# Two transformer blocks on one core: score and meta-key products padded to 128 rows, stick-breaking scores from fp32r parts

## The chip, the cores and the metric

The kernel runs on one core of a Trainium2 chip. The metric is the device time of one execution in microseconds; three executions of the kernel before are given. TensorE is called PE in the profile, its weight loads PEld, VectorE DVE, ScalarE ACT, GpSimd POOL and SyncE SP.

## The reference

512 tokens of 1024 features go through two layers of a first block and one layer of a second one. All is float32.

```python
for l in range(2):                                   # block 1, 16 meta tokens ahead of the 512
    hn = rmsnorm(h, norm_gain[l]); proj = hn @ w_in[l]
    # four heads of two maps (64 features each): a = softmax(q0 k0) - lam * softmax(q1 k1); do = a @ v
    do = rmsnorm(diff_attention(dq, dk, dv, lam, chunk_ids), subln_gain[l]) * (1 - lam_init) * silu(dg)
    # eight heads of 64 features, scores plus cumulated log-sigmoids of a forget gate, causal
    fo = forgetting_attention(fq, fk, fv, cum_logf, positions) * silu(fg)
    h = h + concat([do, fo]) @ w_out[l]
x = rmsnorm(h, final_gain)[:, 16:]
x = x + 0.5 * swiglu(rms_norm(x))                    # block 2
h = rms_norm(x) @ w_in_2
o_nsa = gate0 * compressed + gate1 * selected + gate2 * window    # eight query heads, two key heads
z = q_s @ k_s.T / 8                                  # stick-breaking, eight heads
a = where(mask, exp(log_sigmoid(z) + suffix sums of log_sigmoid(-z)), 0); o_sb = a @ v_s
x = x + concat([o_nsa, o_sb]) @ w_out_2
x = x + memory_cross_attention(rms_norm(x), rms_norm(mem), ...)   # 256 memory rows, four heads
x = x + 0.5 * swiglu(rms_norm(x))
```

At 512 tokens the 8 selection blocks are all selected, so the selected and the window branch are both plain causal attention here.

## The kernel before

Activations lie feature-major in eight tiles `h` of 128 features by tokens. A large product takes both operands in two fp32r parts, high and low, and adds three passes into one bank of PSUM (`dense`, `dense_tok`). The weights come through `Stream`: a DMA on SP's queue, the high part by ScalarE (L131), the low part by VectorE (L132).

Attention is put between the large products by a clock of TensorE work (`mm` and `tr` add to `self.clock`; `at` and `soon` give a step a due time; `poll` and `wait` emit it). `pump` emits one step of attention and asks for the next after a delay in proportion to its cost, at least `MIN_STEP` or `MIN_STEP2`. A step `a` makes the scores of a tile of 128 queries and their exponentials, `b` or `fl` follows about `LAT_AB` later with the transposes on TensorE, `pv` about `LAT_BC` after that with the products with the values. The order that results is scheduled once more against a simulated time line when the program is built, and is then fixed on each engine.

Scores of a head (`qk`) are two fp32r products over operands that `stack` makes. For head h of a pair, the queries are a tile of 128 rows, the high parts in the head's own 64 rows and the low parts in the other 64; the keys are a tile with the high parts in the own 64 rows and the key as it is in the others. The second product adds the high parts of the queries with the low parts of the keys, over the head's own 64 rows alone:

```python
own = slice(64 * h, 64 * h + 64)
q = Q[0][h]
self.mm(out, q[(slice(None), *qc)], K[0][h][(slice(None), *kc)], True, False)
self.mm(out, q[(own, *qc)], K[1][(own, *kc)], False, stop)
```

In block 1 (`layer`) the scores of a query tile have 16 + 128(t+1) keys, at least 256 columns where 128 queries are in work; the tile t = 3 is cut in two halves of 264 (`scores`). The causal masks are added by a bfloat16 product with the identity, the forget gate's sums by a bfloat16 product of `sel` and `ck` over 72 rows. The transposed probabilities of the 16 meta keys stand in a tile `PTm` of 16 rows, the values in `Vm`, and `pv` begins with their product. The mixer does selected and window attention (`nsa_steps`, keys `nk` and `nkl`), then stick-breaking (`sb_steps`). Its scores are one f32 product over 64 rows of the pair's queries and keys (L1501), which runs as two passes; tanh, a reversed running product on VectorE (L1509) and one more VectorE operation (L1511) make the weights. Each pair's steps may begin when its own keys and queries are there. While they run, TensorE also does the output products of the first half of the heads. The attention over the memory (`memory`) uses `qk` with keys `mk` and `mkl` from `memory_operands`.

Of the kernel before, what the change touches and what calls it, by code (L numbers as in the profile page):

```python
# [11 lines left out]
F32 = mybir.dt.float32  # L12
# [28 lines left out]
T = 512  # L41
# [59 lines left out]
def layer_order(l):  # L101
    """products of a layer of block 1 in their order"""
    o = []
    gates = [(u + "g", i) for u, i in UNITS]
    for n, (u, i) in enumerate(UNITS):
        o += [(u + x, i) for x in "vkq"]
        for _ in range((GA0, GA1)[l][n]):
            o.append(gates.pop(0))
    return o + [("o", d) for d in range(KD)]


class Stream:
    """Weights in the order of their use: loaded and split into two float32r parts a few chunks ahead."""
# [30 lines left out]
def weight_plan(A):  # L144
    plan = []

    def cut(key, src, cols, rows=None):
        """[rows, cols] of src"""
# [55 lines left out]
class Prep:  # L204
    """The operands of the products after an rms norm: X = h*gain in two parts, R = 1/rms on every partition."""
# [7 lines left out]
    def split(self, d, a=None, b=None):  # L213
        """X of feature tile d, columns a:b of its tokens"""
# [7 lines left out]
class Net:  # L222
# [14 lines left out]
    # ---- PSUM tiles, one bank each  # L237
# [12 lines left out]
    # ---- order of emission: chains of small steps are placed between the large products by a clock of PE time  # L250
# [4 lines left out]
    def soon(self, delay, pri, fn):  # L255
        """at, with the instructions of fn ahead of their place by pri"""
# [15 lines left out]
    def feed(self, items, interval):  # L272
        """emit items (ready, fn) one after another, each interval(i) after the one before"""
# [17 lines left out]
    # ---- TensorE  # L291
# [17 lines left out]
    def dense(self, ps, m, W, c0, X, seg, ks=None):  # L309
        """ps[m, tokens] = W^T X, three passes over the parts; ks: only these row tiles"""  # L310
# [12 lines left out]
    def dense_tok(self, ps, Ws, c0, n, X, t0):  # L323
        """ps[tokens t0.., n] = X^T W over the chunks Ws of rows"""
# [14 lines left out]
    # ---- small arithmetic  # L339
# [15 lines left out]
    def stacks(self, pool, tag, shape, keys, bufs=2):  # L355
        """tiles for the operands of two heads: queries [high; low], keys [high; high], and the low parts of keys"""
        S = [pool.tile([128, *shape], F32R, tag=f"{tag}{h}", name=f"{tag}{h}", bufs=bufs) for h in range(2)]
        return S, pool.tile([128, *shape], F32R, tag=tag + "l", name=tag + "l", bufs=bufs) if keys else None

    def stack(self, dst, src, cut):  # L360
        """two heads of 64 features of src into the tiles of stacks, at cut(tile)"""
        nc, v = self.nc, self.nc.vector
        S, L = dst
        for h in range(2):
# [5 lines left out]
            v.tensor_tensor(out=cut(S[h])[other] if L is None else cut(L)[own], in0=src[own], in1=hi.bitcast(F32),  # L370
                            op=ALU.subtract)

    def qk(self, out, Q, K, h, qc, kc, stop):
        """out = q k^T for head h, queries qc, keys kc"""
        own = slice(64 * h, 64 * h + 64)
        q = Q[0][h]
        self.mm(out, q[(slice(None), *qc)], K[0][h][(slice(None), *kc)], True, False)
        self.mm(out, q[(own, *qc)], K[1][(own, *kc)], False, stop)

    def rsqrt(self, dst, ms, n, p=128):  # L380
        """dst = 1/sqrt(ms) for [p, n]: a first guess from the bits, a step of third order, one of second"""
# [15 lines left out]
    def colsum(self, ps, parts, chunks, off):  # L397
        """ps[tokens, chunk] = sums over partitions of the parts"""
# [12 lines left out]
    def spread(self, r, chunks, R, off):  # L411
        """R [128, tokens]: r [tokens of a chunk, chunk] on every partition"""
# [10 lines left out]
    # ---- set up: constants, gains, residual  # L423
    def setup(self):
# [21 lines left out]
        with self.tc.tile_pool(name="setup", bufs=1) as sp:  # L446
# [19 lines left out]
            # rms of the tokens of block 1, from the rows as they came  # L466
# [56 lines left out]
            with self.tc.issue_after(self.ins[S_LATE]):  # L523
# [10 lines left out]
                # -lambda of each layer, on every partition  # L534
# [15 lines left out]
    # ---- rms norm of the residual, built up feature tile by feature tile  # L550
# [28 lines left out]
    def norm_end(self, P, token_r=None):  # L579
        """chain of the statistics; token_r: [128, 4] for 1/rms with tokens on partitions"""  # L580
# [50 lines left out]
    # ---- block 1  # L631
    def layer(self, l, P, nxt):
# [5 lines left out]
        with ExitStack() as st:  # L638
# [5 lines left out]
            self.ck = np_.tile([72, TT], BF16, name="ck")  # L644
            swap = list(range(8, 16)) + list(range(0, 8)) + list(range(16, 32))
            done = {}
# [19 lines left out]
            def proj(kind, u, i):  # L666
# [17 lines left out]
                dst = self.stacks(ap, "p" + kind, [TT], kind == "k")  # L684
# [3 lines left out]
            def values(u, i, vT):  # L688
                V = ap.tile([128, 4, 128], F32, tag="V", name="V", bufs=2)
                Vm = ap.tile([16, 128], F32, tag="Vm", name="Vm", bufs=2)  # L690

                def flip_v():
# [6 lines left out]
                    nc.scalar.copy(Vm, ps[:16, :128])  # L699
# [1196 lines left out]
```

## Time and profile before

| | |
|---|---|
| runs | 1974.67, 1979.1, 1981.31 us; median 1979.1 |
| span of the profiled execution, first to last instruction | 1969.9 us |
| its own time | its device time is not given beside the span; the median of the runs is 9.2 us above the span |
| TensorE busy | 1929.5 us (98%), 11075 matmuls |
| weight loads busy | 1553.2 us (79%) |
| VectorE busy | 1159.0 us (59%) |
| ScalarE busy | 846.4 us (43%) |
| GpSimd busy | 0.7 us |
| mean granted TensorE clock | 0.992 |

The stages follow from the names of the tiles: attention of layer 0 from 67 to 374 us, of layer 1 from 453 to 733, the first feed-forward from 857 to 1175, the mixer's projections to 1290, selected and window attention to 1437, stick-breaking to 1516, attention over the memory from 1546 to 1592, the second feed-forward from 1620. In a row of the timeline the columns are start and duration in us, engine, line, operation, output<-inputs, for TensorE rows times columns of the weights, then the moving operand, and a count; an fp32r operand is shown as f32. Matmul durations overlap, since the ends are modelled; the distance of two starts tells what a product keeps TensorE for. In rows of groups by line the columns are busy time, mean duration, idle time before and what ended it. L293 is the call of the matmul in `mm`, L306 the one in `tr`.

### The profile page before, as it was taken

To read this page: it belongs to the slowest core of one execution; us is meant where nothing else is said; L and a number is where in the kernel's file an instruction comes from. 1 tells how busy PE (TensorE), PEld (TensorE's weight loads), DVE (VectorE), ACT (ScalarE), POOL (GpSimd) and SP (SyncE) were. 2 spreads that over 40 slices of the span, in tenths; PEclk is the share of its full clock that TensorE was granted. 3 is DMA by queue.
4 is the path that set the end of the run, shared out by engine and by line. 5 is a ranking of instruction groups with operands and counts; after the bars stand their busy time and mean duration, and the time that the engine had idled before them with its cause. 6 is when DMAs were issued, how large, how long until landed. Compare 5 with 4: busy or idle time off the path is not lost.

```text
span 1969.9 us, 28237 instructions
## 1 busy us (share of the span) xinstructions
PE 1929.5 (98%) x11075; PEld 1553.2 (79%) x11075; DVE 1159.0 (59%) x2637; ACT 846.4 (43%) x1874; POOL 0.7 (0%) x6
## 2 busy tenths in 40 slices
PE   6999999999999999999999999999999999999999
PEld 5888888797888767888888888976665688888887
DVE  4976655458775547663443557865676665344353
ACT  4555565535555555432222233435566443222222
POOL 0000000000000000000000000000000000000000
PEclk9999999999999999999999999999999799999999
DMA  8665541176574312333333335320010123333332
GB/s 140 67 66 50 60 44 44 44 80 69 57 62 59 52 33 81 103 108 96 97 96 94 89 93 162 84 67 23 22 44 12 33 71 89 97 96 96 93 88 87
DMA packets 259439, 145.21 MB, mean 74 GB/s; under 512 B 9242, under 2 KB 256604, under 8 KB 259308
## 3 DMA queue, kind: packets, MB, share of 16 engines
q1 hardware_dynamic: 259308, 143.42, 35.7%
q8 instruction: 87, 1.43, 0.3%
q14 instruction: 44, 0.36, 0.1%
HBM read 141.30 MB, written 2.10 MB: 73 GB/s over the span
## 4 chain that ended last, share of the span: by engine, by line
PE 92%; DMA 4%; DVE 2%; ACT 1%; issue 0%; SPq 0%; DVEq 0%; ACTq 0%
PE mm L293 68%; PE s L293 12%; PE po L293 7%; PE pt L306 5%; DMA w<-in_w_in_dram 2%; PE pt L293 1%; DMA CS<-in_c_shape_dram 1%; DMA xs<-in_x_dram 1%; DVE wlo L132 0%; DMA gc<-in_nsa_kc_norm_dram 0%; DMA gr<-in_ffn_norm_dram 0%; ACT whi L131 0%; ACT L738 0%; DVE rp L661 0%; SPq L1157 0%
## 5 line engine op out<-in xcount | busy, mean ns | idle before, releaser
L131 ACT ACTIVATE whi<-w 128x1024 fp32r<-128x1024 f32 (+2 forms) x253 | 263.1, 1042 | 589.9 <-PE mm L293 504.8
L132 DVE TENSOR_TENSOR wlo<-w,whi 128x1024 fp32r<-128x1024 f32 (+2 forms) x253 | 303.6, 1201 | 76.8 <-ACT whi L131 75.6
L293 PE MATMUL mm<-actl,whi 128*128 128x512 f32 x352 | 139.4, 397 | 0.0
L293 PE MATMUL mm<-acth,wlo 128*128 128x512 f32 x352 | 139.3, 397 | 0.0
L293 PE MATMUL mm<-acth,whi 128*128 128x512 f32 x352 | 139.2, 397 | 0.0
L734 DVE TENSOR_REDUCE nm<-s 128x1 f32<-128x264 f32 (+4 forms) x171 | 69.1, 408 | 79.3 <-PE s L293 78.5
L1090 DVE SCALAR_TENSOR_TENSOR h<-mm,h 128x512 f32<-128x512 f32 x48 | 33.0, 691 | 138.0 <-PE mm L293 138.0
L738 ACT ACTIVATE P<-s,nm 128x264 f32<-128x264 f32 (+4 forms) x171 | 78.0, 458 | 72.6 <-DVE nm L734 47.9
L306 PE MATMUL pt<-ident,P 128*128 128x128 f32 (+2 forms) x588 | 97.6, 277 | 1.8 <-DVE P L1511 1.5
L1078 DVE TENSOR_TENSOR u<-mm,R 128x512 f32<-128x512 f32 x42 | 29.0, 691 | 108.6 <-PE mm L293 108.6
L293 PE MATMUL mm<-cl,whi 128*128 128x264 f32 (+1 forms) x256 | 88.2, 345 | 0.1
L293 PE MATMUL mm<-ch,wlo 128*128 128x264 f32 (+1 forms) x256 | 87.2, 343 | 0.5 <-DVE wlo L132 0.5
L293 PE MATMUL mm<-ch,whi 128*128 128x264 f32 (+1 forms) x256 | 85.8, 350 | 1.3 <-ACT ch L937 0.7
L1071 DVE TENSOR_TENSOR g<-mm,R 128x512 f32<-128x512 f32 x42 | 29.0, 690 | 89.3 <-PE mm L293 89.3
L293 PEld LDWEIGHTS mm<-acth,wlo 128*128 128x128 f32 x352 | 66.4, 189 | 15.9
L293 PEld LDWEIGHTS mm<-actl,whi 128*128 128x128 f32 x352 | 66.4, 189 | 15.9
L293 PEld LDWEIGHTS mm<-acth,whi 128*128 128x128 f32 x352 | 66.4, 189 | 15.8
L293 PE MATMUL mm<-x0h,whi 128*128 128x512 f32 (+1 forms) x202 | 71.7, 355 | 5.0 <-ACT raw L659 3.4
L306 PEld LDWEIGHTS pt<-ident,P 128*128 128x128 f32 (+2 forms) x588 | 60.9, 131 | 18.2 <-issue 13.9
L293 PE MATMUL mm<-x1h,wlo 128*128 128x512 f32 (+1 forms) x202 | 71.6, 355 | 0.0
L293 PE MATMUL mm<-x6h,whi 128*128 128x512 f32 (+1 forms) x202 | 71.0, 352 | 0.0
L293 PE MATMUL mm<-x7h,whi 128*128 128x512 f32 (+1 forms) x202 | 71.0, 352 | 0.0
(702 smaller groups left out, 5258.8 us busy)
## 6 DMA issues: line engine op xcount, KB each, us to landing
w<-in_w_in_dram SPq DMA_DIRECT2D x84, 512.0 KB, 6.8
w<-in_ffn_wg_dram SPq DMA_DIRECT2D x44, 512.0 KB, 4.0
w<-in_ffn_wu_dram SPq DMA_DIRECT2D x44, 512.0 KB, 3.9
w<-in_ffn_wd_dram SPq DMA_DIRECT2D x32, 512.0 KB, 3.7
w<-in_w_out_dram SPq DMA_DIRECT2D x20, 512.0 KB, 3.7
w<-in_ffn_wd_dram SPq DMA_DIRECT2D x16, 384.0 KB, 3.4
xs<-in_x_dram SPq DMA_DIRECT2D x4, 512.0 KB
w1k<-in_cmp_w_k_dram SPq DMA_DIRECT2D x4, 512.0 KB, 6.9
```

The lines of the kernel that those rows point to most:

```text
L131: nc.scalar.activation(out=hi, in_=w, func=AF.Copy)
L132: nc.vector.tensor_tensor(out=lo, in0=w, in1=hi.bitcast(F32), op=ALU.subtract)
L293: self.nc.tensor.matmul(out, lhsT, rhs, start=start, stop=stop)
L306: self.nc.tensor.transpose(out, in_, self.ident[:p, :p])
L734: v.tensor_reduce(out=nm[:nq, c:c + 1], in_=s[:nq, :b - a], axis=AX.X, op=ALU.max, negate=True)
L738: nc.scalar.activation(out=P_[:nq, a:b], in_=S[c][:nq, :b - a], func=AF.Exp, bias=nm[:nq, 0:1], accum_out=ls[:nq, c:c + 1])
L1071: v.tensor_tensor(out=g, in0=pg, in1=R, op=ALU.mult)
L1078: v.tensor_tensor(out=u, in0=pu, in1=R, op=ALU.mult)
L1090: v.scalar_tensor_tensor(out=H[d], in0=ps, scalar=0.25, in1=H[d], op0=ALU.mult, op1=ALU.add)
```

## The change

- `stacks` now makes low parts of keys as two tiles, one for each head of a pair, of 128 rows each (`low_parts`); the 64 rows of the other head are set to zero once by GpSimd (`zero`). `qk` runs both products over all 128 rows.
- In `layer` these tiles, the `Vm` tiles and the `PTm` tiles are made once, two of each in turn, with 128 rows, zeroed at the layer's start; `ck` and `sel` are used with 128 rows instead of 72.
- Stick-breaking scores go through `qk`: `sb_stack` cuts a pair's keys and queries into parts, for the next pair at the second tile of the pair before, for the first pair when the stage begins. There are two sets of six tiles, one in the place of the operands x4 to x6 of the large products. The scores have at least 256 columns. All four pairs now wait for the last pair's projections.
- `dynamic_dma_scratch_size=1024` is given to the program.

Docstrings and comments go too; they are left out here.

```diff
     def stacks(self, pool, tag, shape, keys, bufs=2):
         S = [pool.tile([128, *shape], F32R, tag=f"{tag}{h}", name=f"{tag}{h}", bufs=bufs) for h in range(2)]
-        return S, pool.tile([128, *shape], F32R, tag=tag + "l", name=tag + "l", bufs=bufs) if keys else None
+        return S, self.low_parts(pool, tag, shape) if keys is True else keys or None
+
+    def low_parts(self, pool, tag, shape):
+        L = [pool.tile([128, *shape], F32R, tag=f"{tag}l{h}", name=f"{tag}l{h}", bufs=1) for h in range(2)]
+        for h in range(2):
+            self.zero(L[h][64 - 64 * h:128 - 64 * h])
+        return L
+
+    def zero(self, t):
+        self.nc.gpsimd.memset(t.bitcast(F32) if t.dtype == F32R else t, 0.0)
...
-            v.tensor_tensor(out=cut(S[h])[other] if L is None else cut(L)[own], in0=src[own], in1=hi.bitcast(F32),
+            v.tensor_tensor(out=cut(S[h])[other] if L is None else cut(L[h])[own], in0=src[own], in1=hi.bitcast(F32),
...
     def qk(self, out, Q, K, h, qc, kc, stop):
-        own = slice(64 * h, 64 * h + 64)
-        q = Q[0][h]
-        self.mm(out, q[(slice(None), *qc)], K[0][h][(slice(None), *kc)], True, False)
-        self.mm(out, q[(own, *qc)], K[1][(own, *kc)], False, stop)
+        q, at = Q[0][h][(slice(None), *qc)], (slice(None), *kc)
+        self.mm(out, q, K[0][h][at], True, False)
+        self.mm(out, q, K[1][h][at], False, stop)
...
-            self.ck = np_.tile([72, TT], BF16, name="ck")
+            self.ck = np_.tile([128, TT], BF16, name="ck")
...
+            lows = [self.low_parts(ap, f"pk{a}", [TT]) for a in range(2)]
+            vms = [ap.tile([128, 128], F32, name=f"Vm{a}") for a in range(2)]
+            ptms = [ap.tile([128, 2, 128], F32, name=f"PTm{a}") for a in range(2)]
+            for x in vms + ptms:
+                self.zero(x)
+            done = {"m": 0}
...
-                dst = self.stacks(ap, "p" + kind, [TT], kind == "k")
+                dst = self.stacks(ap, "p" + kind, [TT], lows[UNITS.index((u, i)) % 2] if kind == "k" else None)
...
-                Vm = ap.tile([16, 128], F32, tag="Vm", name="Vm", bufs=2)
+                Vm = vms[UNITS.index((u, i)) % 2]
...
-                    nc.scalar.copy(Vm, ps[:16, :128])
+                    nc.scalar.copy(Vm[:16], ps[:16, :128])
...
-                PTm = ap.tile([16, 2, 128], F32, tag="PTm", name="PTm", bufs=2)
+                PTm = ptms[done["m"] % 2]
+                done["m"] += 1
...
-                nc.scalar.copy(PTm[:, :nq], psm[:16, o:o + nq])
+                nc.scalar.copy(PTm[:16, :nq], psm[:16, o:o + nq])
...
-                    P_, ls = scores(qT, kT, hh, t, self.masks[:, 1], self.sel[:72, 2 * i + hh, :], f"P{hh}",
+                    P_, ls = scores(qT, kT, hh, t, self.masks[:, 1], self.sel[:, 2 * i + hh, :], f"P{hh}",
...
-            kS, qS = {}, {}
+            kS, qS, sets, stacked = {}, {}, [], {}
+
+            def sb_stack(p):
+                if not sets:
+                    for a in range(2):
+                        pool, tags = (self.xp, ("x4h", "x4l", "x5h", "x5l", "x6h", "x6l")) if a == 0 else \
+                            (done["tp"], [f"sb{x}" for x in range(6)])
+                        x = [pool.tile([128, T], F32R, tag=tag, name="sbs" + str(n), bufs=1) for n, tag in enumerate(tags)]
+                        for h in range(2):
+                            self.zero(x[4 + h][64 - 64 * h:128 - 64 * h])
+                        sets.append(((x[0:2], None), (x[2:4], x[4:6])))
+                Q, K = sets[p % 2]
+                self.stack(K, kS[p], lambda x: x)
+                self.stack(Q, qS[p], lambda x: x)
+                stacked[p] = Q, K
...
                 def a(t, hf):
                     n = 128 * (t + 1)
                     qc = slice(128 * t, 128 * t + 128)
-                    rows = slice(64 * hf, 64 * hf + 64)
                     s = self.ps_s()
-                    self.mm(s[:, :n], qS[p][rows, qc], kS[p][rows, :n], True, False)
+                    if t == 1 and hf == 0 and p < 3:
+                        sb_stack(p + 1)
+                    w = max(n, 256)
+                    self.qk(s[:, :w], *stacked[p], hf, [qc], [slice(0, w)], False)
...
-                    [(lambda p=p: p in qS and "tp" in done, p, sb_steps) for p in range(4)]
+                    [(lambda: 3 in qS and "tp" in done, p, sb_steps) for p in range(4)]
...
                     if make is sb_steps and i == 0:
                         done["wait"] = True
+                        sb_stack(0)
...
-    nc = bacc.Bacc("TRN2", target_bir_lowering=False, num_devices=1)
+    nc = bacc.Bacc("TRN2", target_bir_lowering=False, num_devices=1, dynamic_dma_scratch_size=1024)
```

More of the change, by code (lines that the diff above doesn't have):

```diff
@@ L643, in layer @@
             CR, SR = CS[:, 0], CS[:, 1]
-            self.ck = np_.tile([72, TT], BF16, name="ck")
+            self.ck = np_.tile([128, TT], BF16, name="ck")
             swap = list(range(8, 16)) + list(range(0, 8)) + list(range(16, 32))
-            done = {}
+            lows = [self.low_parts(ap, f"pk{a}", [TT]) for a in range(2)]
[4 more added lines that the diff above has]
+            done = {"m": 0}
             att = {}
```

## The prediction

> **What bounds the kernel now.** The page first: its span line and engine totals; then the chain that ended last, summed by line; then busy time by stage.
>
> ```profile
> span 1969.9 us, 28237 instructions
> PE 1929.5 (98%) x11075; PEld 1553.2 (79%) x11075; DVE 1159.0 (59%) x2637; ACT 846.4 (43%) x1874; POOL 0.7 (0%) x6
> ```
>
> ```profile
> by line: PE mm L293 67.6%; PE s L293 11.7%; PE po L293 6.8%; PE pt L306 5.1%; DMA w<-in_w_in_dram 2.3%; PE pt L293 0.7%; DMA CS<-in_c_shape_dram 0.6%; DMA xs<-in_x_dram 0.5%; DVE wlo L132 0.5%; issue 0.4%; DMA gc<-in_nsa_kc_norm_dram 0.3%;
> ```
>
> ```profile
> 67.00:374.00 307.00, 305.90 (x2246) 258.17 (x2244) 193.44 (x538) 170.93 (x510) 0.00 (x0) 1.00 0.44 52
> 453.00:733.00 280.00, 278.61 (x1748) 221.93 (x1746) 184.53 (x451) 153.87 (x412) 0.00 (x0) 1.00 0.47 56
> 1290.00:1437.00 147.00, 146.68 (x898) 100.04 (x897) 93.18 (x253) 76.53 (x208) 0.00 (x0) 1.00 0.12 33
> 1437.00:1516.00 79.00, 76.10 (x454) 45.47 (x454) 56.97 (x119) 47.30 (x110) 0.00 (x0) 1.00 0.09 27
> 1546.00:1592.00 46.00, 42.00 (x249) 32.23 (x249) 34.16 (x109) 25.73 (x73) 0.00 (x0) 0.78 0.01 2
> ```
>
> TensorE is on the chain for about 92% of the span (the PE entries added up, most of them products on L293). The five stage rows (length, then PE, PEld, DVE, ACT, POOL busy, clock, DMA) are the attention of layer 0, of layer 1, the selected-and-window attention, the stick-breaking attention and the attention over the memory. In the first three TensorE has no holes, VectorE is busy 63%, 66% and 63%, ScalarE 56%, 55% and 52%. So time taken off a TensorE instruction there comes off the span, until a chain through VectorE and ScalarE is late.
>
> A busy TensorE is not one at its peak, so I read the spacing of its starts, from the timeline (start, busy, then the instruction).
>
> ```profile
> 454.50 0.28 PE L293 MATMUL mm<-x7h,wlo 128*128 128x264 f32 x1
> 454.62 0.28 PE L293 MATMUL s<-pk,pq 128*128 128x256 f32 x1
> 454.82 0.38 PE L293 MATMUL s<-pkl,pq 64*128 64x256 f32 x1
> 455.14 0.23 PE L293 MATMUL s<-masks,identb 128*128 128x128 bf16 x1
> ```
>
> ```profile
> 272.89 0.39 PE L293 MATMUL s<-pkl,pq 64*128 64x264 f32 x1
> 273.20 0.29 PE L293 MATMUL s<-ck,sel 72*128 72x264 bf16 x1
> 273.24 0.37 PE L293 MATMUL s<-pk,pq 128*128 128x264 f32 x1
> 273.55 0.39 PE L293 MATMUL s<-pkl,pq 64*128 64x264 f32 x1
> 273.86 0.29 PE L293 MATMUL s<-ck,sel 72*128 72x264 bf16 x1
> 273.99 0.22 PE L293 MATMUL s<-masks,identb 128*128 128x128 bf16 x1
> ```
>
> A full-height product of 264 columns is followed after 0.12 us (454.50 to 454.62). A product that has a 64-row one behind it is followed after 0.20 (454.62 to 454.82), and the 64-row product itself after 0.32 (to 455.14; 0.31 from 273.55 to 273.86). The same price from one stretch: from 272.89 to 273.55 three products of 264 columns take 0.66 us, where three at 0.12 would take 0.36 to 0.37. So going to 64 rows and back costs 0.29 us a pair (0.08 to 0.09 in, 0.20 out). The 72-row product costs nothing of the kind: 0.13 us from 273.86 to 273.99. Where the score product follows a short one, the spacing behind it is 0.31 (273.24 to 273.55); I don't count the extra 0.11, since it comes from the short spacing ahead of it.
>
> **The change part by part.** The profile's time is the span of 1969.9; the runs have a median of 1979.1 (1974.67 to 1981.31), so 9.2 us lie between span and median. I subtract from the span and take the same amount off the median.
>
> *Low-part score products, 64 to 128 rows.* Block 1 has 2 layers x 8 units x 2 heads x 5 products with 256 columns or more = 160. The mixer has 64.
>
> ```profile
> L293 PE MATMUL s<-pkl,pq x171: 179/386/452, 67.0 to 733.2; 64*128 64x264 f32 x62, 64*128 64x256 f32 x31, 64*128 64x272 f32 x31, 64*128 64x400 f32 x31
> L293 PE MATMUL s<-nkl,nq x64: 377/411/502, 1290.5 to 1434.4; 64*128 64x256 f32 x32, 64*128 64x384 f32 x16, 64*128 64x512 f32 x16
> L293 PE MATMUL po<-PTm,Vm x144: 203/268/320, 249.6 to 752.0; 16*64 16x128 f32 x128, 16*64 16x16 f32 x16
> L293 PE MATMUL po<-Vm,PTm x72: 267/274/373, 78.2 to 623.2; 16*128 16x128 f32 x64, 16*16 16x128 f32 x8
> ```
>
> (155 of the 160 are in the first row, the other five go to a buffer of another name.) 160 x 0.29 = 46 us, 64 x 0.29 = 19 us. The number of columns does not change, so the product costs what a full-height one costs, 0.12. Bounds of a pair: nothing, if the spacing is not due to the height, and 0.38, if the 0.11 above goes too. I take 0.29, measured between like products. The 16-column pairs of the meta queries I put at 0.
>
> *Meta-key products, 16 to 128 rows.* 72 and 144 instructions; those with 128 columns are two passes of 32 and 64 products.
>
> ```profile
> 106.30 0.48 PE L293 MATMUL po<-Vm,PTm 16*128 16x128 f32 x2
> 106.71 0.94 PE L293 MATMUL po<-V,PT 128*128 128x128 f32 x6
> 107.40 0.37 PE L293 MATMUL mm<-x1l,whi 128*128 128x264 f32 x1
> ```
>
> ```profile
> 271.62 0.43 PE L293 MATMUL po<-PTm,Vm 16*64 16x128 f32 x2
> 271.98 0.66 PE L293 MATMUL po<-PT,V 128*64 128x128 f32 x8
> 272.57 0.39 PE L293 MATMUL s<-pk,pq 128*128 128x264 f32 x1
> ```
>
> Heads of two maps: the two passes take 0.41 (106.30 to 106.71); the six full-height ones behind them take 0.69 (to 107.40), 0.115 each, so two would take 0.23. With 0.09 for the way in, taken as for the 64 rows, 0.27 is saved, x 32 = 9 us. Forgetting heads have two such groups a tile, of which one stands ahead of full-height passes as here: 0.36 for two passes, against eight full-height ones in 0.59, 0.15 for two. That saves 0.21 a tile, x 32 = 7 us. The other group stands alone, and its half-width output would still change the shape of the array on both sides; I count nothing for it. Ends 0.1 and 0.4 a tile, 3 and 13 us. Together 16.
>
> *The bias product, 72 to 128 rows:* 0, by the 0.13 above. *Scratch size of dynamic DMA:* the program issues no such DMA from POOL; 0.
>
> *Stick-breaking scores.* 32 products of two f32 passes on 64 rows become 32 pairs of fp32r products of max(n, 256) columns.
>
> ```profile
> 1453.94 0.49 PE L293 MATMUL s<-sbk,sbq 64*128 64x128 f32 x2
> 1454.36 0.23 PE L293 MATMUL s<-masks,identb 128*128 128x128 bf16 x1
> ```
>
> ```profile
> 1448.07 1.12 PE L293 MATMUL s<-sbk,sbq 64*128 64x512 f32 x2
> 1449.12 0.23 PE L293 MATMUL s<-masks,identb 128*128 128x128 bf16 x1
> ```
>
> ```profile
> L367 ACT ACTIVATE mk<-mkT x2: 626/628/630, 1445.0 to 1445.7; 64x512 fp32r<-64x512 f32 x2
> L369 DVE CAST mk<-mkT x2: 422/422/423, 1445.0 to 1445.5; 64x512 fp32r<-64x512 f32 x2
> L370 DVE TENSOR_TENSOR mkl<-mkT,mk x2: 684/686/689, 1446.0 to 1446.7; 64x512 fp32r<-64x512 f32 x2
> ```
>
> ```profile
> L1406 DVE SCALAR_TENSOR_TENSOR sbk<-mm,R x4: 690/692/692, 1281.1 to 1326.0; 128x512 f32<-128x512 f32 x4
> ```
>
> Before, 0.42 us at 128 columns and 1.05 at 512; in between evenly, 0.63 and 0.84. After, twice 0.12 at 256 columns, and in proportion 0.18 and 0.24 at 384 and 512: 0.24, 0.24, 0.36, 0.48. The difference over the four tiles is 1.62, x 8 = 13 us, and the way into 64 rows adds 0.09 x 32 = 3: 16 us of TensorE time. But each of the 4 pairs now needs its operands cut: 4 casts on ScalarE (0.63), 2 copies (0.42) and 4 subtractions (0.69) on VectorE, priced by the memory's keys of the same shape: 2.5 and 3.6 us a pair, 10 and 14 us in all. VectorE is busy 57 of this stage's 79 us; with 14 more it needs 71, and 79 - 16 = 63 aren't enough. VectorE is late next, behind its scan and products, and the score products of the next pair wait for its subtractions. I put the stage at 75, a gain of 4; ends +16 (the cuts all lie in slack) and -8 (all 24 us of cuts lie in the way, less the 16). That the first pair now waits for the projections of all four costs nothing: keys and queries are made from 1281 to 1326 on, the first scores stand at 1437.
>
> *Attention over the memory:* 16 pairs, 4.6 us at 0.29.
>
> ```profile
> 1558.06 0.58 PE L293 MATMUL s<-mk,mq 128*128 128x256 f32 x1 [3.70 <-ACT Pm L1773]
> 1558.57 0.58 PE L293 MATMUL s<-mkl,mq 64*128 64x256 f32 x1
> ```
>
> ```profile
> PE s L293 <- ACT P L738: 1.7, 2, 1.4
> ```
>
> ```profile
> masks.py:197 POOL MEMSET ident<- 128x128 f32 x1 | 0.2, 204 | 0.3 <-POOLq L1884 0.3
> ```
>
> The first eight pairs end in a wait of 3.70 us for ScalarE, which eats what they save. The other eight run at the halved clock (0.51 between starts). I take 3, between 0 and 10.
>
> *Zeros on POOL:* 8 fills a layer, 2 and 2 for the other keys, 4 for stick-breaking, 24 in all. By 0.2 us for 128 columns a fill of 528 is under 1 us, so under 24 us on an engine that is busy 0.7 us and on which nothing else waits. The cover is the projections and weights ahead of each first score; without it a layer starts 1 to 2 us later. I take 0.
>
> *What is late next in blocks 1 and 2.* The steps are issued at fixed distances of TensorE work, and these shrink by 11 to 13% ((46 + 16) of 587, 19 of 147). VectorE would then be busy about 71%. At present TensorE waits little for softmax (1.7 us for the exponentials in both layers). I take 5 us of new waits, between 0 and 25.
>
> Sum: 46 + 19 + 16 + 4 + 3 - 5 = 83. Span 1969.9 - 83 = 1887; median 1979 - 83 = 1896.
>
> **The rivals.**
>
> *The chains take over.* The attention stages become bound by the way from scores over maximum, exponential and scaling back to the transposes, and half of the gain is lost: 1979 - 42 = 1937. For it: VectorE at 63% and more, and distances in the code that go with the slower TensorE. Against it: waits of a few us in 587 us of block 1's attention.
>
> *The padded product pays for its weights in the open.* A full-height product may hide its weight load less than assumed, say by another 0.09 at each of the two products. Then a pair saves 0.11, the meta products half: 25 + 8 + 4 + 3 - 1 = 39, time 1940. Against it: full-height products, each with its own weights, stand at 0.12 (454.50 to 454.62). The Trainium skill, page "TensorE: Matmul & The Clock Gate", section "Part 3: Packing small matmuls — row/col tiling", says that a weight load overlaps running matmuls only when the row groups differ; by that rule this rival would win, but the spacing of 0.12 speaks against it here.
>
> *It does not do what it says.* If the spacing comes from the accumulation or the short operands and not from the height, only stick-breaking changes: 1975, no change within what can be told (0.3%, 6 us).
>
> *Slower: the clock.* In the memory stage the mean granted clock is 0.78, and products of 256 columns stand 0.51 apart. Were the padded products, half of whose rows are zeros, to halve the clock in layer 0's attention, each us of TensorE work there would take 2; it decides from 83 us of such work on. With half of the stage's remaining 276 us it gives 1979 - 83 + 138 = 2034. Against it: the clock is 1.00 in the four stages before the memory, with 64-row products that fill half the array as well.
>
> **How the numbers follow.** Forecast 0.73, chains 0.13, weights 0.06, no effect 0.04, clock 0.04. Everything at its better end: 46 + 19 + 22 + 16 + 10 = 113, so 1866; I set the low end at 1868. The high end of 1940 takes in the two rivals that halve the gain. Faster by over 0.3%: 0.73 + 0.13 + 0.06 = 0.92; same 0.04; slower 0.04.
>
> **What would show it.** No 64-row form of the low-part products; 0.12 behind each of them at 264 columns. Layer stages near 275 and 250 us, the next near 128, stick-breaking near 75 with VectorE above 90%. PE waits for exponentials under 5 us in each layer. Wrong: spacings of 0.2 or more behind the padded products, or TensorE holes in the attention stages that add up to over 25 us.

## The result, and the profile after

| | before | after |
|---|---|---|
| median of the runs | 1979.15 us (1974.67 to 1981.31) | 1889.95 us (1888.62 to 1890.34) |
| ratio, with its 95% interval | | 0.9555 [0.9536, 0.9574] |
| span of the profiled execution | 1969.9 us | 1886.5 us |
| mean granted clock | 0.992 | 0.992 |

The forecast was 1896, range 1868 to 1940. The span fell by 83.4 us, the forecast's sum was 83. The median fell by 89, since the profiled execution of before took less than the median. After's profiled execution took 1888.62 us, 2.1 above its span; by the same distance the one of before would have taken about 1972.0, less than any of its runs shown.

Where the 83 us come from, stage by stage. A stage begins with its first score product on TensorE, layer 1 and stick-breaking where the row above them ends; it ends with the start of its last product of one kind. For a layer and the memory that is the last output product (a layer is attention and the products around it), for selected and window attention the last score product, for stick-breaking the last product with the values. "Mixer start" goes from the last product of the first feed-forward to the first compression product. Columns to the right are the experiments below that move most.

| us | before | after | forecast of the difference | measured | only scores padded | only meta padded | stick-breaking as before | cuts once |
|---|---|---|---|---|---|---|---|---|
| start | 66.9 | 68.4 | 0 | +1.5 | 68.2 | 67.3 | 67.8 | 67.4 |
| layer 0 | 351.6 | 321.0 | both layers: -57 | -30.6 | 327.9 | 344.5 | 320.6 | 319.9 |
| layer 1 | 366.2 | 334.6 | | -31.6 | 345.2 | 358.7 | 334.9 | 334.9 |
| mixer start | 31.0 | 26.4 | 0 | -4.6 | 26.4 | 29.5 | 26.4 | 26.4 |
| selected and window | 143.9 | 132.8 | -19 | -11.1 | 126.7 | 143.8 | 126.7 | 127.4 |
| stick-breaking | 81.9 | 80.7 | -4 | -1.2 | 81.6 | 81.9 | 81.7 | 72.6 |
| memory | 44.6 | 38.6 | -3 | -6.0 | 37.0 | 46.0 | 37.3 | 38.8 |

The rest (two feed-forwards, the mixer's other products, the output products) is within 0.2 us of before in after's profile. The new waits of the forecast, 5 us, are taken into the row of the layers.

The page after: the span and the engine totals.

```profile
span 1886.5 us, 28324 instructions
PE 1836.1 (97%) x11075; PEld 1535.6 (81%) x11075; DVE 1167.3 (62%) x2661; ACT 851.0 (45%) x1890; POOL 12.0 (1%) x30
```

As many matmuls as before keep TensorE busy 93 us less. Busy time by stage, the five stages in the order of the prediction (length, then PE, PEld, DVE, ACT, POOL, clock, DMA):

```profile
68.40:345.10 276.70, 272.86 (x2246) 249.86 (x2244) 191.00 (x537) 168.40 (x508) 0.00 (x0) 1.00 0.49 57
423.60:673.30 249.70, 247.47 (x1745) 215.58 (x1744) 182.38 (x450) 152.50 (x411) 0.00 (x0) 1.00 0.52 63
1225.00:1357.80 132.80, 130.03 (x868) 95.42 (x866) 97.16 (x259) 77.96 (x210) 2.27 (x4) 0.99 0.13 37
1357.80:1438.50 80.70, 72.73 (x484) 50.27 (x483) 65.96 (x137) 53.16 (x124) 1.21 (x2) 0.96 0.08 27
1469.30:1507.90 38.60, 31.90 (x238) 26.94 (x238) 32.58 (x107) 24.51 (x71) 0.00 (x0) 0.91 0.00 1
```

The layer stages have almost no holes: TensorE is idle for 3.8 and 2.2 us in them, with VectorE at 69% and 73%. Stick-breaking has 8 us of idle TensorE and a clock below 1. The padded pair, from the timeline of layer 1, and the meta-key passes from that of layer 0:

```profile
424.54 0.28 PE L293 MATMUL mm<-x7h,wlo 128*128 128x264 f32 x1
424.65 0.28 PE L293 MATMUL s<-pk,pq 128*128 128x256 f32 x1
424.77 0.28 PE L293 MATMUL s<-pk0l,pq 128*128 128x256 f32 x1
424.89 0.23 PE L293 MATMUL s<-masks,identb 128*128 128x128 bf16 x1
```

```profile
104.80 0.39 PE L293 MATMUL po<-Vm,PTm 128*128 128x128 f32 x2
105.03 0.83 PE L293 MATMUL po<-V,PT 128*128 128x128 f32 x6
```

The starts stand 0.12 apart on both sides of the low-part product, where they stood 0.20 and 0.32 apart before. The two meta passes take 0.23 (104.80 to 105.03) instead of 0.41. Both numbers are those of the forecast.

### The profile page after: what moved, and what is told of

It is laid out like the page before. It is cut to its first block, busy times and chain, and to the rows that moved or that the text cites. A ratio compares the mean times of both kernels' runs of the same rounds, so it can differ in the third digit from the quotient of the medians.

```text
span 1886.5 us, 28324 instructions
## 1 busy us (share of the span) xinstructions
PE 1836.1 (97%) x11075; PEld 1535.6 (81%) x11075; DVE 1167.3 (62%) x2661; ACT 851.0 (45%) x1890; POOL 12.0 (1%) x30
## 4 chain that ended last, share of the span: by engine, by line
PE 88%; DMA 4%; DVE 4%; ACT 2%; issue 1%; SPq 0%; DVEq 0%; ACTq 0%
PE mm L293 69%; PE s L293 8%; PE po L293 6%; PE pt L306 5%; DMA w<-in_w_in_dram 3%; PE pt L293 1%; DMA CS<-in_c_shape_dram 1%; DVE wlo L132 1%; ACT whi L131 0%; ACT sbs L377 0%; DVE sc L1542 0%; DVE P L1544 0%; ACT Pm L1807 0%; DMA mw<-in_mem_wq_dram 0%; ACT PT L1454 0%
## 5 line engine op out<-in xcount | busy, mean ns | idle before, releaser
L132 DVE TENSOR_TENSOR wlo<-w,whi 128x1024 fp32r<-128x1024 f32 (+2 forms) x253 | 303.6, 1202 | 81.6 <-ACT whi L131 80.2
L749 DVE TENSOR_REDUCE nm<-s 128x1 f32<-128x264 f32 (+4 forms) x171 | 67.8, 406 | 41.8 <-PE s L293 40.1
L306 PEld LDWEIGHTS pt<-ident,P 128*128 128x128 f32 (+2 forms) x588 | 62.2, 133 | 25.0 <-issue 14.4
L293 PEld LDWEIGHTS mm<-acth,wlo 128*128 128x128 f32 x352 | 66.3, 188 | 16.0
L293 PEld LDWEIGHTS mm<-actl,whi 128*128 128x128 f32 x352 | 66.3, 188 | 16.0
L293 PEld LDWEIGHTS mm<-acth,whi 128*128 128x128 f32 x352 | 66.3, 188 | 15.9
L293 PE MATMUL mm<-x5h,whi 128*128 128x512 f32 (+1 forms) x202 | 71.0, 352 | 0.0
```

The costliest lines, as they stand in the source:

```text
L132: nc.vector.tensor_tensor(out=lo, in0=w, in1=hi.bitcast(F32), op=ALU.subtract)
L293: self.nc.tensor.matmul(out, lhsT, rhs, start=start, stop=stop)
L306: self.nc.tensor.transpose(out, in_, self.ident[:p, :p])
L749: v.tensor_reduce(out=nm[:nq, c:c + 1], in_=s[:nq, :b - a], axis=AX.X, op=ALU.max, negate=True)
```

## The experiments

**Low-part scores alone.** The changed kernel with the meta-key products on 16 rows, the bias on 72 and the stick-breaking scores as before; the smaller scratch stays.

```diff
-            vms = [ap.tile([128, 128], F32, name=f"Vm{a}") for a in range(2)]
...
-                    self.qk(s[:, :w], *stacked[p], hf, [qc], [slice(0, w)], False)
+                    self.mm(s[:, :n], qS[p][rows, qc], kS[p][rows, :n], True, False)
```

> The low-part score products of all three attentions padded to 128 rows (and the scratch size, without which the tiles have no room), the meta products on 16 rows and the stick-breaking scores as before. Theory, the array's change of shape costs 0.29 us a pair: layers 0 and 1 together 46 us shorter (attention about 284 and 257 us), selected-and-window attention 17 to 19 shorter (no cuts of stick-breaking operands lie in it), memory 6; in all about 70, 1905 to 1912 us. Rival, the changed kernel's gain comes from the cheaper stick-breaking and the meta products and only half from here: 1940.

Measured: 1899.11 us, 0.9605 [0.9590, 0.9619]. The layers lose 23.7 and 21.0 us, the selected and window attention 17.2, memory 7.6, the mixer's start 4.6. The scores give what their 0.29 a pair promised; the total came out lower than expected through memory and the mixer's start.

**Meta-key products alone,** on the kernel before. The bias product stays on 72 rows, other than the expectation says.

```diff
-                Vm = ap.tile([16, 128], F32, tag="Vm", name="Vm", bufs=2)
+                Vm = vms[UNITS.index((u, i)) % 2]
```

> The kernel before with the meta-key products (and the bias product) on 128 rows, all else as before. Theory: 0.27 us a tile for heads of two maps, 0.2 for forgetting heads, 16 us over the two layers, 1963 us, nothing in the later stages. Rival, these short products lie in gaps between others: under 5 us, 1975 or more.

Measured: 1960.29 us, 0.9910 [0.9896, 0.9925]; the layers lose 7.1 and 7.5 us, 14.6 together.

**All but the stick-breaking part.** The changed kernel, its stick-breaking scores as one f32 product over 64 rows again, without cuts.

```diff
-                    if t == 1 and hf == 0 and p < 3:
-                        sb_stack(p + 1)
...
-                    self.qk(s[:, :w], *stacked[p], hf, [qc], [slice(0, w)], False)
+                    self.mm(s[:, :n], qS[p][rows, qc], kS[p][rows, :n], True, False)
```

> The changed kernel with the stick-breaking scores as before (f32, 64 rows, no cuts). Theory, the cuts of the first two pairs, which stand in the middle of the selected-and-window attention, cost there what the stage fell short of (about 6 us), and the stick-breaking stage gained only 1: this is 4 to 6 us faster than the changed kernel, 1884 to 1886, with the selected-and-window stage at 127 and stick-breaking at 82. Rival, the fp32r scores are worth their 16 us and the stage was kept up by something else: 1895 to 1905.

Measured: 1883.15 us, 0.9523 [0.9509, 0.9537], 4 us below the changed kernel of the later comparison (1887.22) and 7 below the first. Selected and window attention, then stick-breaking:

```profile
1224.28:1350.97 126.69, 126.21 (x869) 93.93 (x867) 89.86 (x247) 72.97 (x202) 0.00 (x0) 1.00 0.14 38
1350.97:1432.69 81.72, 78.82 (x484) 47.52 (x483) 59.23 (x125) 49.59 (x116) 1.47 (x2) 1.00 0.08 26
```

Without the cuts the first of the two takes 6.1 us less than after, the second 1.0 more: the stick-breaking part of the change costs 5 us net.

**Scratch size alone,** on the kernel before.

```diff
-    nc = bacc.Bacc("TRN2", target_bir_lowering=False, num_devices=1)
+    nc = bacc.Bacc("TRN2", target_bir_lowering=False, num_devices=1, dynamic_dma_scratch_size=1024)
```

> The kernel before with the smaller scratch and nothing else. The start of the mixer became 4.5 us shorter in the changed kernel: six small loads of gains no longer stand on SP's queue ahead of the compression weights. Theory, that comes from where tiles lie in memory, and the scratch size alone moves them: 4 to 5 us faster, 1975, mixer start 113. Rival, it comes from the padded tiles or the order: no difference, 1979.

Measured: 1971.67 us, 0.9969 [0.9957, 0.9982]. The mixer starts in 26.4 us instead of 31.0. The kernel before first: the load of a gain row, `gq`, with an issue of `w_in` behind it on SP's queue, from the timeline, and ScalarE's wait for `w_in`, its longest in this stretch:

```profile
1173.52 0.34 SPq L1157 DMA_DIRECT2D gq<-in_nsa_q_norm_dram  x1
...
1183.35 1.60 SPq L128 DMA_DIRECT2D w<-in_w_in_dram  x2
```

```profile
ACT whi L131 <- DMA w<-in_w_in_dram: 8.8, 1, 8.8
```

The load with this edit, from the rows of its tile, and the same wait:

```profile
L1157 SPq DMA_DIRECT2D gq<-in_nsa_q_norm_dram x1: 340/340/340, 878.9 to 878.9; - x1
```

```profile
ACT whi L131 <- DMA w<-in_w_in_dram: 4.6, 1, 4.6
```

Before, six gain-row loads stand on the queue from 1173.5 on, ahead of the compression weights and of the next chunk of `w_in`, for which ScalarE waits 8.8 us. With the smaller scratch `gq` is loaded at 878.9, and that wait is 4.6. That its tile no longer waits for another tile's place would explain it, but no run here shows it.

**The changed kernel again,** beside the next three.

> The changed kernel again, as the measure for the runs beside it: 1890 us, ratio 0.955.

Measured: 1887.22 us, 0.9555 [0.9539, 0.9571].

**Cuts held back.** The cuts of the first pair are issued after an exponential and a reciprocal late in the window attention, the others after the first stick-breaking tile.

```diff
+                ma, mv = mark[min(p, 1)]
+                with self.tc.issue_after(ma), self.tc.issue_after(mv):
-                self.stack(K, kS[p], lambda x: x)
-                self.stack(Q, qS[p], lambda x: x)
+                    self.stack(K, kS[p], lambda x: x)
+                    self.stack(Q, qS[p], lambda x: x)
```

> The changed kernel with the cuts of the first pair held on ScalarE and VectorE until the fourth-last steps of the selected-and-window attention, and those of the second pair until the first stick-breaking step. Theory, twenty cuts in a row delayed the softmax chains of the selected-and-window attention: that stage falls from 133 to 127 or 129, the stick-breaking stage stays at 81 or gains 1 to 2 of it back: 1885 to 1888. Rival, the cuts cost the same wherever they lie, since VectorE is the bound of both stages: 1890.

Measured: 1887.63 us, 0.9554 [0.9540, 0.9568], no gain over the changed kernel. The stages:

```profile
1225.14:1355.09 129.95, 127.57 (x865) 94.62 (x864) 92.73 (x252) 75.00 (x206) 2.07 (x4) 0.99 0.13 37
1355.09:1439.30 84.21, 72.30 (x489) 48.84 (x487) 69.12 (x144) 55.54 (x129) 1.04 (x2) 0.98 0.08 26
```

2.9 us leave the first stage and 3.5 enter the second, where the theory had no loss. The cost was moved, not saved, which is what the rival said of the total.

**Cuts once.** Only the first pair is cut, and its parts serve all four pairs, so three pairs score with another pair's operands; the products are those of the changed kernel.

```diff
-                    if t == 1 and hf == 0 and p < 3:
-                        sb_stack(p + 1)
...
-                    self.qk(s[:, :w], *stacked[p], hf, [qc], [slice(0, w)], False)
+                    self.qk(s[:, :w], *stacked[0], hf, [qc], [slice(0, w)], False)
```

> The changed kernel with the operands of the first pair alone cut and used for all four pairs (three pairs score with the wrong operands). Takes away 7.5 us of ScalarE and 11 us of VectorE work and one set's zeros. Theory, VectorE bounds stick-breaking: the stage falls from 81 to 72 or 74, the one before by 3: 1879. Rival, the stage is set by the distances at which its steps are issued and the chain through the scan: stage 78 or more, 1885 to 1887.

Measured: 1875.18 us, 0.9493 [0.9479, 0.9507]. Stick-breaking:

```profile
1350.46:1423.09 72.63, 68.61 (x485) 47.83 (x483) 58.36 (x125) 47.98 (x116) 1.21 (x2) 1.00 0.09 30
```

Against the row with the old scores, TensorE is busy 10 us less and the stage is 9.1 us shorter. So the fp32r products themselves gain 9 us, and the cuts take back 8 in this stage (80.7 against 72.6) and 5 to 6 in the one ahead of it.

**Cuts on GpSimd:** copies and subtractions there, casts on ScalarE as they were.

```diff
-                self.stack(K, kS[p], lambda x: x)
+                self.stack(K, kS[p], lambda x: x, nc.gpsimd)
```

> The changed kernel with the copies and subtractions of the stick-breaking cuts on GpSimd, which is idle, in place of VectorE; ScalarE's casts stay. Theory, VectorE bounds stick-breaking and was late in the stage before: 14 us off VectorE, stages 130 and 75, 1882. Rival, GpSimd takes over 1.5 us for each (its fill of 64x512 took 0.6 us) and the first scores wait for it, or it slows VectorE: 1890 or more.

Measured: 1884.55 us, 0.9541 [0.9526, 0.9555], between the two expectations. The stage ahead takes 128.5 us instead of 132.8, as the theory had it, but stick-breaking 84.5 instead of 80.7. Its groups on GpSimd and on VectorE, where the second pair of lines is the changed kernel:

```profile
L380 POOL TENSOR_TENSOR sbs<-sbk,sbs 64x512 fp32r<-64x512 f32 x8 | 11.7, 1468 | 0.6
L1542 DVE TENSOR_TENSOR_SCAN sc<-P,ones 128x128 f32<-128x128 f32 (+3 forms) x32 | 27.7, 876 | 14.2 <-ACT P L1541 13.9
L1544 DVE SCALAR_TENSOR_TENSOR P<-P,sc 128x128 f32<-128x128 f32 (+3 forms) x32 | 17.1, 544 | 1.4
```

```profile
L1542 DVE TENSOR_TENSOR_SCAN sc<-P,ones 128x128 f32<-128x128 f32 (+3 forms) x32 | 25.7, 820 | 8.9 <-ACT P L1541 8.6
L1544 DVE SCALAR_TENSOR_TENSOR P<-P,sc 128x128 f32<-128x128 f32 (+3 forms) x32 | 15.1, 485 | 1.3
```

A subtraction takes about twice as long on GpSimd as on VectorE (1.47 us on the mean against 0.69), and VectorE's own scans and products grow by 2 us each in sum. The growth sits in few of them, which run beside a subtraction on GpSimd; from the timelines of both engines:

```profile
1375.97 1.48 POOL L380 TENSOR_TENSOR sbs<-sbq,sbs 64x512 fp32r<-64x512 f32 x1
1376.23 2.30 DVE L1542 TENSOR_TENSOR_SCAN sc<-P,ones 128x512 f32<-128x512 f32 x1
```

A scan of 512 columns takes 1.22 us otherwise. This scan, a second one (1.96) and two products (1.64 where 0.56 is usual, 1.51 where 0.68 is) hold nearly all of the growth. Two stretches at about half clock go with it, where the changed kernel has one:

```profile
1387.00:1392.00 5.00, 5.00 (x25) 3.77 (x23) 2.92 (x6) 2.98 (x9) 0.00 (x0) 0.53 0.30 104
1407.00:1412.00 5.00, 5.00 (x22) 3.53 (x21) 3.55 (x7) 2.57 (x7) 0.00 (x0) 0.50 0.00 0
```

How much of the 3.8 us each of these takes was not separated.

**Memory on 64 rows:** the changed kernel with the memory's low-part products as before.

```diff
-        self.mm(out, q, K[1][h][at], False, stop)
+        self.mm(out, Q[0][h][(rows, *qc)], K[1][h][(rows, *kc)], False, stop)
```

> The changed kernel with the low-part products of the memory attention over 64 rows again. In the kernel before the clock halved for 20 us in this stage, in the changed one it did not fall below 0.91 of full on average. Theory, it is the spaced 64-row products that let it fall: the clock is near 0.77 again, the stage 44 to 45 us instead of 38.6, 1896. Rival, the fall depends on TensorE's wait for the first exponentials and on chance: stage 40 to 41 (0.29 us for the eight later pairs), 1892, clock 0.9.

Measured: 1896.93 us, 0.9606 [0.9590, 0.9622]. The memory stage is back at 46.1 us, with a mean clock of 0.74; the rival's 40 to 41 at 0.9 is out. First this kernel's stretch after the scores begin, then the kernel before at the same place, then the changed kernel with the product that ends its hole, then a row of the second profile of the changed kernel:

```profile
1473.00:1477.00 4.00, 4.00 (x12) 2.51 (x11) 2.89 (x8) 0.06 (x1) 0.00 (x0) 0.51 0.00 0
```

```profile
1548.00:1552.00 4.00, 4.00 (x19) 2.81 (x19) 3.81 (x10) 0.53 (x1) 0.00 (x0) 0.95 0.00 0
...
1568.00:1572.00 4.00, 4.00 (x22) 3.34 (x22) 1.84 (x5) 2.60 (x9) 0.00 (x0) 0.50 0.01 2
```

```profile
1471.00:1475.00 4.00, 2.29 (x15) 1.67 (x14) 3.81 (x12) 0.15 (x1) 0.00 (x0) 1.00 0.00 0
1475.00:1479.00 4.00, 0.00 (x0) 0.00 (x0) 3.22 (x20) 1.74 (x7) 0.00 (x0) 0.89 0.02 4
1479.00:1483.00 4.00, 3.93 (x18) 3.60 (x20) 3.60 (x13) 3.71 (x14) 0.00 (x0) 0.50 0.00 0
```

```profile
1479.07 0.58 PE L293 MATMUL s<-mk,mq 128*128 128x256 f32 x1 [4.65 <-ACT Pm L1807]
```

```profile
1472.00:1476.00 4.00, 1.90 (x8) 1.61 (x8) 3.94 (x19) 0.00 (x0) 0.00 (x0) 0.56 0.00 0
```

The clock halves in all of them. With 64-row products it halves while the pairs run, and TensorE's rows show no hole (4.00 of 4.00). That does not mean that TensorE works throughout: before the fall the products of the pairs start 0.31 us apart (1547.25, 1547.57 and 1547.88 in the kernel before), the padded ones 0.12. With padded pairs the first profile has the pairs at 1.00 and the fall in the hole of 4.65 us behind them; in the second it comes at about 1472.5, with pairs still in work, behind holes of 0.75 and 0.38 us. So the height does not decide whether the clock falls. What goes with it is how long the clock stays low: 20 to 24 us in the traces of the five kernels with 64-row pairs, 3 to 10 us in the nine profiles with padded ones. The Trainium skill, page "TensorE: Matmul & The Clock Gate", section "Part 1: The HAM clock gate (the "warmup" mystery)", has the clock fall after an idle window of about 3.4 us. The hole in the changed kernel's first profile agrees with it. Its second profile and the 64-row pairs show no such window of idle rows; whether the time between products that start 0.31 us apart counts as idle, or half an array as partly idle, no run here shows.

**A second low-part product.** In block 1 the low-part product of the tiles of 128 queries is issued twice: on 128 rows in the changed kernel, on 64 in the kernel before. The low part is thereby added twice.

```diff
+        if twice:
+            self.mm(out, q, K[1][h][at], False, False)
         self.mm(out, q, K[1][h][at], False, stop)
```

> The changed kernel with each low-part product of block 1 with 128 queries issued twice (the second adds the same once more): 160 more products on 128 rows. All theories: 0.12 to 0.18 us each, 21 us, layers about 288 and 260 us.

> The kernel before with each low-part product of block 1 with 128 queries issued twice, over 64 rows both. Theory A, a change of shape empties the array, once in and once out: the second 64-row product adds 0.13 us like any other, 21 us in all, layers 317 and 290. Theory B, each product that isn't of full height shows its weight load: 0.22 to 0.24 (the second f32 pass of the stick-breaking scores has 0.53 at 512 columns where 0.43 are streamed), 37 us, layers 325 and 298. Theory C, the whole 0.29 belongs to the product: 0.42 each, 67 us, layers 340 and 313.

Measured in one execution each: 1906.33 us on 128 rows; the layers grow by 8.6 and 11.6 us against the changed kernel, 20 us for 160 products, 0.13 each. On 64 rows 1994.73 us; 11.7 and 10.7 us more than before, 22 us, 0.14 each. These are the whole layers. The attention rows alone, in which the expectations are given, are 283.2 and 267.2 us on 128 rows and 316.3 and 297.1 on 64, and the last would fit theory B; but in layer 1 attention then takes in other products too, 1864 where it had 1745, and only 80 of these 119 are new. The timelines, 128 rows first:

```profile
449.60 0.29 PE L293 MATMUL s<-pk,pq 128*128 128x264 f32 x1
449.72 0.41 PE L293 MATMUL s<-pk0l,pq 128*128 128x264 f32 x2
449.97 0.40 PE L293 MATMUL mm<-x3l,whi 128*128 128x512 f32 x1
```

```profile
482.08 0.28 PE L293 MATMUL s<-pk,pq 128*128 128x264 f32 x1
482.29 0.51 PE L293 MATMUL s<-pkl,pq 64*128 64x264 f32 x2
482.73 0.50 PE L293 MATMUL mm<-x3l,whi 128*128 128x512 f32 x1
```

Two 64-row products take 0.44 (482.29 to 482.73), one took 0.31 before: the second costs 0.13, like any product of this width. What was expensive is the change of shape, once in (0.21 to 482.29, where 0.12 is usual) and once out. The Trainium skill, page "TensorEngine Tiling (Array Packing)", section "Key Properties", says that a change of tiling mode drains TensorE; the trace agrees, with 0.29 us for the way in and out.

**Height without cuts.** After these the stick-breaking scores were tried as one f32 product over 128 rows: the queries as they are, each head's keys copied beside 64 rows of zeros.

```diff
+                v.tensor_copy(K[0][0:64], kS[p][0:64])
+                nc.scalar.copy(K[1][64:128], kS[p][64:128])
...
-                    self.qk(s[:, :w], *stacked[p], hf, [qc], [slice(0, w)], False)
+                    self.mm(s[:, :n], qS[p][:, qc], stacked[p][hf][:, :n], True, False)
```

> The changed kernel with the stick-breaking scores as one f32 product again, but over all 128 rows: the queries of the pair as they are, the keys of each head copied (one copy on VectorE, one on ScalarE a pair) into a tile whose other 64 rows are zero. No parts are cut. Theory (what the changed kernel loses in this stage are the cuts; the height alone is worth 32 x 0.29 = 9 us): selected and window attention at 126.7 to 127.5 us as with the stick-breaking scores left as before, stick-breaking at 73 to 75 (81.7 there), total 7 to 9 us below 1883, so 1874 to 1876. Rival (the stage hangs on the chain through tanh, the running product and the transposes, and 72.6 us with one cut alone came from the scores being early): stick-breaking at 79 or more, total 1880 or more.

Measured: 1880.93 us, 0.9524 [0.9509, 0.9539], not told apart from the kernel with the old scores (0.9523). Selected and window attention and stick-breaking as rows of the windows, and one product with what follows from the timeline:

```profile
1226.32:1353.02 126.70, 126.23 (x868) 93.91 (x866) 90.77 (x249) 74.28 (x204) 2.38 (x4) 1.00 0.14 38
1353.02:1431.10 78.08, 75.34 (x484) 48.90 (x483) 60.20 (x127) 50.45 (x118) 1.21 (x2) 1.00 0.09 28
```

```profile
1365.63 1.02 PE L293 MATMUL s<-sbz,sbq 128*128 128x512 f32 x2
1366.48 0.22 PE L293 MATMUL s<-masks,identb 128*128 128x128 bf16 x1
```

Stick-breaking falls by 3.6 us, neither the 7 to 9 of the theory nor nothing. A product of 512 columns still takes 0.85 where it took 1.05: the height gives 0.2 on the way out, and TensorE's busy time falls by 3.5 us only. By difference, the other part of the 9 us came from the fp32r passes, which this version does not have. In the total the 3.6 us are not seen: layer 1 took 3.0 us more in this execution. Here, too, the first pair waits for the projections of all four, and the stage ahead takes 126.7 us as without that wait.

## Why the prediction was right, and where its terms were off

**Spacing, not busy time, priced the change, and that held.** The layers' 62 us less 5 of waits were forecast; they lost 62.2 us with 3.6 us more of idle TensorE than before (6.1 against 2.5, from the stage rows). The low-part scores alone gave 44.7, forecast 46; between the kernel with padded meta-key products alone and the one with only the stick-breaking scores left as before lie 47.7. The meta-key products gave 14.6 by themselves, and 17.6 lie between the kernel with the scores alone and that same one; forecast 16. Both differences also hold the bias product, which was not run alone. The stages stand at 276.7 and 249.7, forecast 275 and 250. PE's waits for exponentials in both layers:

```profile
PE s L293 <- ACT P L753: 3.1, 3, 2.2
```

So the rival of the chains (half of the gain, 42 us, lost) is out. One sign that the prediction named for being wrong, TensorE holes of over 25 us in the attention stages, came close: the five stage rows add up to 23.5 us, 9.7 before, and 8.0 of the 23.5 lie in stick-breaking. The doubled products support the cause of the price, a change of shape, against the rival in which height is not the reason.

**The rival of the weights in the open is out.** The padded products stand at 0.12. The rule of the Trainium skill that was named with it, that a weight load overlaps only when the row groups differ, does not show here: consecutive full-height products with their own weights keep 0.12.

**The slower rival is out:** the clock is 1.00 in both layers. Where the clock did matter, in memory, the padding raised the stage's mean (0.91 against 0.74 with the 64-row products put back).

**The stick-breaking term was mis-sized: +4 forecast, -5 measured.** The step that failed is the cost of the cuts. "VectorE is late next, behind its scan and products" places all of them in the stick-breaking stage; the 19 us of the stage ahead have no term for them. That the first pair waits for the projections of all four did cost nothing (126.7 us with and without that wait). But the cuts of the first two pairs run in the window attention, as soon as their operands are there (rows of the cuts, then the stage's slice, then TensorE's waits):

```profile
L377 ACT ACTIVATE sbs<-sbq x4: 627/632/635, 1262.0 to 1265.7; 64x512 fp32r<-64x512 f32 x4
L380 DVE TENSOR_TENSOR sbs<-sbk,sbs x4: 682/686/690, 1265.4 to 1272.0; 64x512 fp32r<-64x512 f32 x4
```

```profile
1265.00:1285.00 20.00, 17.39 (x105) 10.71 (x103) 15.37 (x33) 11.86 (x29) 1.04 (x2) 0.91 0.09 27
```

```profile
PE pt L306 <- ACT PT L1454: 1.5, 1, 1.5
```

Of two pairs, 8 casts on ScalarE and 12 operations on VectorE stand among the softmax of the window attention. TensorE idles 2.6 of the 20 us from 1265 on, at a clock of 0.91; in the second profile of this kernel the stage takes 132.4 us at 1.00, so the clock is not the reason. The selected and window attention lost 11 us and not the 17.2 that it lost with the old scores; the other 1.8 of the 19 forecast were missing there too. With one pair's cuts alone the stage takes 127.4 us, 0.7 more than without cuts, so most of the 6.1 us come with the second pair's. Where cuts stand matters as well: held back to the end of the stage, one pair's cost 3.3 us (129.95).

In the stick-breaking stage the gain and the cost of the forecast were both there and both smaller: 9 us gained, forecast 16, and 8 lost, forecast 12. A pair of 256-column products takes 0.34 us (1384.33 to 1384.67) where the forecast took 0.24. And the bound was not VectorE's sum over the stage: it is busy 82% (65.96 of 80.70), not above 90%. The third pair's cuts stand on VectorE from 1377 to 1383, ahead of the stick-breaking weights that TensorE waits for; VectorE, busy 4.91 of the 5 us up to 1385, is late after them, and the hole in TensorE that follows is paid twice, since the clock then halves:

```profile
PE pt L306 <- DVE P L1544: 4.0, 3, 2.3
```

```profile
1385.00:1390.00 5.00, 2.35 (x11) 1.51 (x10) 5.00 (x9) 1.73 (x4) 0.00 (x0) 0.94 0.31 105
1390.00:1395.00 5.00, 4.94 (x27) 3.48 (x27) 3.45 (x12) 2.16 (x6) 0.00 (x0) 0.50 0.31 105
```

From 1385 to 1390 VectorE is busy without a break (5.00) and TensorE 2.35 us; then TensorE runs 5 us at half clock. The stage's clock is below 1.00 in the six profiles with all four pairs cut (0.92 to 0.98) and 1.00 in those with one pair cut or none.

**Memory: 3 forecast, 6.0 measured** (7.5 by the kernel with 64 rows there). The forecast took the halved clock as given; with the padding the clock is low for some 7 us of the stage (1478 to 1485 in the first profile) and no longer for some 20.

**Scratch size: 0 forecast, 4.6 measured.** That "the program issues no such DMA" was no reason for 0: the smaller scratch alone moves the load of the gain rows ahead. How it does so stays open.

**Zeros: 11.3 us on GpSimd** (12.0 less 0.7), forecast under 24. Layer 0 starts 1.5 us later than before; starts without the 24 fills were 66.3 and 67.3 in two other kernels, so at most some 2 us are theirs.

So the errors nearly cancel: 8 us short in the selected and window attention, 3 in stick-breaking and 1.5 at the start, against 5 more in the layers, 4.6 at the mixer and 3 in memory. The total was right to 0.4 us of span by this luck, while the largest terms were right for the stated reason.

## What to carry to other kernels

Price a product by the distance of starts on both sides of it, in the same trace: a product over fewer rows may be cheap itself and cost its neighbours a change of shape, which a pad with zeros removes. When a change adds operations to an engine with slack, ask at what time the scheduler can place them, not only in which stage they are needed; here cuts ran in the stage ahead, among a softmax that had no room for them. A version without the costly part is worth its run: leaving the stick-breaking scores as they were gave 0.9523 where the whole change gave 0.9555.

## What the runs showed of the hardware that was not expected

- The granted clock can halve while TensorE's rows show no hole: in memory with 64-row products, 0.51 over 4.00 busy us. It stays low for 20 to 24 us there, with zero-padded rows for 3 to 10 us.
- A hole of 2.3 us in stick-breaking is followed by 5 us at 0.50, that is 2.5 us of lost work by estimate, so it costs about twice its length.
- A second 64-row product behind the first costs 0.13 us, the first 0.41 with the way in and out.
- Beside a subtraction on GpSimd a scan on VectorE took 2.30 us where 1.22 is usual; the mean over all 32 scans goes from 820 to 876 ns, that of the products from 485 to 544.
- Less scratch for DMAs that the program never issues moved a load from 1173.5 to 878.9 us.
